# A decoder trunk on one core: the first group's products taken from x unscaled, its weights reordered, and some loads moved to ScalarE's queue

## The chip, the cores and the metric

The kernel runs on one core of a Trainium2 chip. The metric is the device time of one execution in microseconds (us). TensorE (PE) multiplies, VectorE (DVE) and ScalarE (ACT) do elementwise work, GpSimd (POOL) does a little, and SyncE (SP) issues nearly all transfers. Each engine takes its own instructions in order and waits by semaphore for what other engines and transfers give it. A transfer is issued by an engine's queue and runs on the core's 16 DMA engines.

## The reference

Two layers on x of 256 rows by 1024 columns in float32: a gated feed-forward, a mixer (pooling in the first layer, attention in the second) and a second gated feed-forward, each between two RMS norms. What is at issue here is the very first piece:

```python
def rms_norm(x, gain):
    y = x32 * lax.rsqrt(jnp.mean(x32 * x32, axis=-1, keepdims=True) + RMS_EPS) * gain
def swiglu(h, w_gate, w_up, w_down):
    return (jax.nn.silu(h @ w_gate) * (h @ w_up)) @ w_down
...
f = swiglu(rms_norm(h, g[0]), ffn_w_gate[0, 0], ffn_w_up[0, 0], ffn_w_down[0, 0])   # h = x at first
```

The norm's factor, one number for each row, can be put on the rows of x before the product or on the rows of the product after it. The gain belongs to a column of x and must be in before the product.

## The kernel before

The 256 rows are two tiles of 128 (i = 0, 1). Every float32 operand is cut into a high part (a cast to fp32r, on ScalarE) and a low part (the rest, a subtraction on VectorE); a product is three matmuls: high by high, high by low, low by high. Weights come as blocks of 1 MB, `ws[b]`, in two halves of 128x1024; a half is a "unit" and holds two K chunks of 128 rows by 512 columns. Blocks 0 and 1 are the first 512 columns of the gate's weights (units 0 to 3, for K chunks 0 to 7), blocks 2 and 3 the same columns of up's (units 4 to 7). So the first group has 2 row tiles x 8 units x 6 = 96 matmuls into four accumulators.

`opening` (L622) does this group. It puts a hand-written order on PE, DVE, ACT and SP (`manual_schedule`, L695): within an engine its instructions run as they stand in the text. Work that stands behind the block in the text is placed by the compiler's scheduler, which may slip it in between where it sees an engine idle.

- `keep_warm` (L86) issues small matmuls on zeros. WARM at L90, the four FILL at L713 to L730.
- SP's order: x tile 0, first 512 columns (L74), the first gain (L92), x tile 1, first half (L703), unit 0 in two pieces of 512 columns (L707), unit 1 (L102), the second halves of x (L710), blocks 1 and 2 (L711); block 3 when a raw buffer is free (L758). There are three raw buffers.
- For each row tile `size_x` (L634) takes the largest of 128 values of a row (L636), floors it (L639) and inverts it (L640). `rows` multiplies a half of x by that, on DVE for the first half (L645) and on ACT for the second (L647).
- `turn_gain` (L649) turns the gain into a column for each K chunk. `turn_x` (L654) transposes four K chunks of a row tile on PE, `scaled_x` (L660) multiplies them by the gain on DVE, `high_x` (L668, ACT) and `low_x` (L671, DVE) make the two parts.
- `high` (L674, ACT) and `low` (L683, DVE) make a unit's parts. Units 0 and 1 lie in the two buffers of `xyp`, the six others in the six of `hlp`.
- `products` (L687) issues the matmuls of one unit and row tile: H is high by high, X low x by high weights, W high x by low weights; each has two entries, for the unit's two K chunks.
- `rstd_of` (L198) takes the norm's factor: four squares with a sum on ACT (L193), L195 on DVE, a power on POOL. L775 multiplies it with the size again, and the gate and up read that as `q` (L304, L313).
- Behind the block come the sums for a Strassen-like scheme (L779 to L787, parts at L272 and L273), then the gate (L304) behind a table load, and then `pair` (L365): `load_form` casts its first block (`us`, L368: ACT L117, DVE L118, both 128x2048), PE multiplies it (tile g), two `xy` blocks are loaded and added (L363), and so on.

Of the kernel before, what the change touches and what calls it, by code (L numbers as in the profile page):

```python
# [19 lines left out]
P = 128  # L20
# [12 lines left out]
WARM = 26  # L33
FILL = 9, 5, 8, 4
LEAST = 1e-3
SIZE_OF = 128
# [17 lines left out]
def trunk_kernel(ctx: ExitStack, tc: tile.TileContext, x, pos, gains, pscale, ws, wq, invf, amask, pmat, icnt, out):  # L54
# [37 lines left out]
    nc.sync.dma_start(gfirst[0:KC, 0:P], gains[0].rearrange("(k p) -> k p", p=P))  # L92
# [525 lines left out]
    q0 = cp.tile([P, 2], F32, name="q_x")  # L618
# [3 lines left out]
    def opening():  # L622
# [3 lines left out]
        size = cp.tile([P, 2], F32, name="size_x")  # L626
        over = cp.tile([P, 2], F32, name="over_x")
        raws, highs, units, t, tps = [], [], [], {}, {}
        banks = [accp.tile([P, 512], F32, tag="acc", name=f"acc_b0{k}") for k in range(4)]
        gu = [banks[0::2], banks[1::2]]  # L630
        y = [sc4.tile([P, D], F32, tag="y", name=f"n_x{i}") for i in range(2)]
        H, X, W = [(0, 0, 0), (0, 1, 0)], [(1, 0, 0), (1, 1, 0)], [(0, 0, 1), (0, 1, 1)]

        def size_x(i):  # L634
            z = slice(i, i + 1)
            nc.vector.tensor_reduce(  # L636
                size[:, z], h[i][:, :SIZE_OF], axis=mybir.AxisListType.X, op=ALU.max, apply_absolute_value=True
            )
            nc.vector.tensor_scalar(size[:, z], size[:, z], LEAST, None, op0=ALU.max)  # L639
            nc.vector.reciprocal(over[:, z], size[:, z])  # L640

        def rows(i, b):
            c, z = slice(b * 512, (b + 1) * 512), slice(i, i + 1)
            if b == 0:
                nc.vector.tensor_scalar_mul(y[i][:, c], h[i][:, c], over[:, z])  # L645
            else:
                nc.scalar.mul(y[i][:, c], h[i][:, c], over[:, z])  # L647

        def turn_gain():  # L649
            tp = tpp.tile([P, 4, P], F32, tag="tp", name="tp_gain")  # L650
            nc.tensor.transpose(tp[:, 0, :KC], gfirst[:KC, :P], ident[:KC, :KC])
            nc.scalar.copy(gcol, tp[:, 0, :KC])

        def turn_x(i, b):  # L654
            tps[i, b] = tp = tpp.tile([P, 4, P], F32, tag="tp", name=f"tp_x{i}{b}")
            for c in range(4):
                k = b * 4 + c
                nc.tensor.transpose(tp[:, c], y[i][:, k * P : (k + 1) * P], ident)
# [15 lines left out]
        def high(j, k=None):  # L674

            if j == len(highs):
                pool, tag = (xyp, "xy") if j < 2 else (hlp, "hl")
                highs.append(pool.tile([P, 2, 1024], F32R, tag=tag, name="hl"))
                units.append((highs[j][:, 0], highs[j][:, 1]))
# [15 lines left out]
        with tc.manual_schedule(  # L695
# [8 lines left out]
            raw = rawp.tile([P, 2, 1024], F32, tag="raw", name="raw0")  # L704
            for k in range(2):
                c = slice(k * 512, (k + 1) * 512)
                nc.sync.dma_start(raw[:, 0, c], ws[0, :, c])  # L707
            raws.append(load_raw(raw=raw, at=1))
            for i in range(2):
                nc.sync.dma_start(h[i][:, 512:], x[i * P : (i + 1) * P, 512:])  # L710
            raws.extend(load_raw() for _ in range(2))  # L711
            turn_gain()
            keep_warm(FILL[0])  # L713
            size_x(0)
            rows(0, 0)
            turn_x(0, 0)
            size_x(1)
            rows(1, 0)
            scaled_x(0, 0)
            keep_warm(FILL[1])  # L720
            turn_x(1, 0)
            scaled_x(1, 0)
            keep_warm(FILL[2])
            high(0, 0)
            high_x(0, 0)
            high(0, 1)
            low(0, 0)
            products(0, 0, H)
            low_x(0, 0)
            keep_warm(FILL[3])  # L730
            high_x(1, 0)
            products(1, 0, H[:1])
            products(0, 0, W[:1], X)
            low(0, 1)
            products(1, 0, H[1:], W[:1])
            products(0, 0, W[1:])
            products(1, 0, W[1:])
            low_x(1, 0)
            high(1)
            rows(0, 1)  # L740
            rows(1, 1)
            low(1)
            products(1, 0, X)
            turn_x(0, 1)
            for i in range(2):
                products(i, 1, H, X)
            turn_x(1, 1)
            for i in range(2):
                products(i, 1, W)
            high(2)  # L750
            scaled_x(0, 1)
            high_x(0, 1)
# [578 lines left out]
```

## Time and profile before

| what | value |
|---|---|
| time, three runs | 946.73, 946.79, 949.97 us (median 946.79) |
| profiled execution: time, span | 947.89 us, 946.1 us |
| PE busy | 930.6 us (98%), 4513 matmuls |
| DVE busy, ACT busy, POOL busy | 744.5 us, 565.2 us, 41.3 us |
| granted TensorE clock, mean | 0.998 |

The span is what the profiler saw between the first and the last instruction; the time of the same execution is 1.8 us longer. Busy PE includes overlap of neighbouring matmuls, so idle time is better read from what an engine waits for than from the share.

### The profile page before, as it was taken

To read this page: it belongs to the slowest core of one execution; us is meant where nothing else is said; L and a number is where in the kernel's file an instruction comes from. 1 tells how busy PE (TensorE), PEld (TensorE's weight loads), DVE (VectorE), ACT (ScalarE), POOL (GpSimd) and SP (SyncE) were. 2 spreads that over 40 slices of the span, in tenths; PEclk is the share of its full clock that TensorE was granted. 3 is DMA by queue.
4 is the path that set the end of the run, shared out by engine and by line. 5 is a ranking of instruction groups with operands and counts; after the bars stand their busy time and mean duration, and the time that the engine had idled before them with its cause. 6 is when DMAs were issued, how large, how long until landed. Compare 5 with 4: busy or idle time off the path is not lost.

```text
span 946.1 us, 12009 instructions
## 1 busy us (share of the span) xinstructions
PE 930.6 (98%) x4513; PEld 767.8 (81%) x4513; DVE 744.5 (79%) x822; ACT 565.2 (60%) x692; POOL 41.3 (4%) x66
## 2 busy tenths in 40 slices
PE   8999999999999999999999999999999999999997
PEld 6878878878888888888888888888899778888885
DVE  6978897789877889878888874686187877888965
ACT  6675674656647576466657653554366766676652
POOL 1000000000100000001000000110000000000000
PEclk9999999999999999999999999999999999999999
DMA  8786976775567698675696875475333545959571
GB/s 306 255 263 199 318 260 178 266 228 201 174 197 255 217 298 267 192 250 188 167 328 156 311 248 196 147 238 171 112 103 132 191 144 167 343 134 374 152 209 44
DMA packets 56777, 202.92 MB, mean 214 GB/s; under 512 B 7496, under 2 KB 7504, under 8 KB 53904
## 3 DMA queue, kind: packets, MB, share of 16 engines
q1 hardware_dynamic: 53472, 178.83, 52.7%
q0 software_dynamic: 3248, 23.33, 12.8%
q8 instruction: 35, 0.57, 0.2%
q14 instruction: 22, 0.18, 0.0%
HBM read 178.02 MB, written 1.05 MB: 189 GB/s over the span
## 4 chain that ended last, share of the span: by engine, by line
PE 84%; DVE 7%; issue 3%; DMA 3%; ACT 2%; SPq 0%; POOL 0%; DVEq 0%; POOLq 0%; ACTq 0%
PE g L140 13%; PE st L341 12%; PE acc_d L471 12%; PE acc_b L140 7%; PE u L140 7%; PE acc_d L140 5%; PE qp L140 4%; PE kp L140 3%; PE q L341 3%; PE vp L140 3%; DMA raw<-in_ws 3%; PE acc_w L140 2%; PE acc_d L341 2%; PE acc_u L140 2%; DVE hl L111 2%
## 5 line engine op out<-in xcount | busy, mean ns | idle before, releaser
L110 ACT CAST hl<-raw 128x1024 fp32r<-128x1024 f32 x146 | 151.6, 1051 | 98.0 <-PE acc_d L140 21.9
L111 DVE TENSOR_TENSOR hl<-raw,hl 128x1024 fp32r<-128x1024 f32 x146 | 176.4, 1220 | 40.2 <-ACT hl L110 38.9
L118 DVE TENSOR_TENSOR hl_lo<-xy,hl_hi 128x2048 fp32r<-128x2048 f32 x55 | 125.9, 2290 | 63.0 <-ACT hl_hi L117 63.0
L117 ACT CAST hl_hi<-xy 128x2048 fp32r<-128x2048 f32 x55 | 105.2, 1913 | 71.0 <-PE u L140 28.2
L118 DVE TENSOR_TENSOR hl_lo<-raw,hl_hi 128x2048 fp32r<-128x2048 f32 x54 | 123.5, 2286 | 17.8 <-ACT hl_hi L117 17.6
L471 PE MATMUL acc_d<-hl,h 128*128 128x512 f32 x576 | 136.9, 392 | 0.0
L471 PEld LDWEIGHTS acc_d<-hl,h 128*128 128x128 f32 x576 | 107.2, 188 | 23.5 <-DVE acc_d L530 0.9
L117 ACT CAST hl_hi<-raw 128x2048 fp32r<-128x2048 f32 x54 | 103.3, 1913 | 26.6 <-PE st L341 9.8
L322 ACT CAST h<-htp 128x512 fp32r<-128x512 f32 (+1 forms) x48 | 26.4, 550 | 33.0 <-PE htp L320 33.0
L140 PE MATMUL acc_b<-hl,aT_m 128*128 128x512 f32 x192 | 44.8, 391 | 0.4 <-ACT aT_m L230 0.2
L140 PE MATMUL acc_d<-hl,h 128*128 128x512 f32 x192 | 44.6, 391 | 0.0
L140 PEld LDWEIGHTS acc_b<-hl,aT_m 128*128 128x128 f32 x192 | 35.7, 188 | 8.3 <-DVE aT_m L231 0.6
L341 PE MATMUL st<-hl_hi,S_m 128*128 128x512 f32 x128 | 41.9, 393 | 0.0
L140 PE MATMUL g<-hl_hi,aT_m 128*128 128x512 f32 x128 | 41.9, 393 | 0.0
L140 PE MATMUL u<-hl_hi,aT_m 128*128 128x512 f32 x128 | 41.8, 393 | 0.0
L140 PEld LDWEIGHTS acc_d<-hl,h 128*128 128x128 f32 x192 | 35.7, 188 | 7.3
L361 POOL DMA_DIRECT2D xy<-raw x22 | 19.2, 872 | 450.6 <-DVE hl_lo L118 161.2
L140 PE MATMUL qp<-hl,aT_f 128*128 128x384 f32 x192 | 37.3, 343 | 0.0
L323 DVE TENSOR_TENSOR h<-htp,h 128x512 fp32r<-128x512 f32 (+1 forms) x48 | 30.8, 641 | 4.9 <-ACT h L322 4.6
L140 PE MATMUL kp<-hl,aT_hk 128*128 128x512 f32 x144 | 34.5, 394 | 0.0
L140 PEld LDWEIGHTS qp<-hl,aT_f 128*128 128x128 f32 x192 | 32.9, 188 | 1.3 <-issue 0.9
L140 PE MATMUL vp<-hl,aT_hk 128*128 128x512 f32 x144 | 33.1, 390 | 0.0
(314 smaller groups left out, 1834.3 us busy)
## 6 DMA issues: line engine op xcount, KB each, us to landing
raw<-in_ws SPq DMA_DIRECT2D x265, 512.0 KB, 4.9
xy<-in_ws SPq DMA_DIRECT2D x44, 512.0 KB, 7.5
xy<-raw POOLq DMA_DIRECT2D x22, 1024.0 KB, 8.3
rawq<-in_wq SPq DMA_DIRECT2D x8, 768.0 KB, 4.7
gain_post<-in_gains SPq DMA_DIRECT2D x14, 256.0 KB, 7.1
gain_pre<-in_gains SPq DMA_DIRECT2D x10, 256.0 KB, 7.3
h<-in_x SPq DMA_DIRECT2D x4, 256.0 KB, 5.5
rawpm<-in_pmat SPq DMA_DIRECT2D x2, 512.0 KB, 4.6
```

The source lines that it names most:

```text
L110: nc.scalar.copy(hl[:, 0, :n], raw[:, k, :n])
L111: last["dve"] = nc.vector.tensor_sub(hl[:, 1, :n], raw[:, k, :n], hl[:, 0, :n])
L117: nc.scalar.copy(hi, raw)
L118: last["dve"] = nc.vector.tensor_sub(lo, raw, hi)
L140: last["mm"] = nc.tensor.matmul(o, l, r, start=start, stop=stop)
L322: nc.scalar.copy(d[:, 0], tp[:, :nt])
L323: nc.vector.tensor_sub(d[:, 1], tp[:, :nt], d[:, 0])
L341: nc.tensor.matmul(ps, a(z, k), u[v], start=start and k == 0 and n == 0, stop=k == 3 and n == 2, skip_group_check=not start,)
L361: nc.gpsimd.dma_start(dst, src, accum_op=ALU.add)
L471: nc.tensor.matmul(f[i][k], d[:, z], u[v][:, r], start=c == 0 and m == 0, stop=m == 2 and (own is not None or c == NF - 1), skip_group_che ...
```

## The change

The sizes and the row multiplications go, with their tiles; `turn_x` transposes x itself, and the norm's whole factor `rx` is handed to the feed-forward as `q`. The gain and the two pieces of unit 0 are issued from ScalarE's queue. Block 2 is loaded before block 1, and the order of the products is units 0, 1, 4, 5, 2, 3, 6, 7: first all that needs K chunks 0 to 3. The gain's transpose takes its PSUM buffer from another pool.

```diff
-WARM = 26
-FILL = 9, 5, 8, 4
+WARM = 22
+FILL = 7, 9, 2, 2
...
-    nc.sync.dma_start(gfirst[0:KC, 0:P], gains[0].rearrange("(k p) -> k p", p=P))
+    nc.scalar.dma_start(gfirst[0:KC, 0:P], gains[0].rearrange("(k p) -> k p", p=P))
...
-        def size_x(i):
-        def rows(i, b):
...
+        def load(b):
+            raws[b] = rawp.tile([P, 2, 1024], F32, tag="raw", name=f"raw{b}")
+            for k in range(2):
+                last["dma"] = nc.sync.dma_start(raws[b][:, k], ws[b, :, k * 1024 : (k + 1) * 1024])
...
-                nc.tensor.transpose(tp[:, c], y[i][:, k * P : (k + 1) * P], ident)
+                nc.tensor.transpose(tp[:, c], h[i][:, k * P : (k + 1) * P], ident)
...
             nc.sync.dma_start(h[1][:, :512], x[P:, :512])
+            raws[0] = rawp.tile([P, 2, 1024], F32, tag="raw", name="raw0")
+            for queue, lo, hi in ((nc.scalar, 0, 512), (nc.scalar, 512, 1024), (nc.sync, 1024, 2048)):
+                queue.dma_start(raws[0].rearrange("p k n -> p (k n)")[:, lo:hi], ws[0, :, lo:hi])
+            load(2)
             for i in range(2):
                 nc.sync.dma_start(h[i][:, 512:], x[i * P : (i + 1) * P, 512:])
+            load(1)
             turn_gain()
+            turn_x(0, 0)
             keep_warm(FILL[0])
             scaled_x(0, 0)
+            high_x(0, 0)
             turn_x(1, 0)
             scaled_x(1, 0)
+            keep_warm(FILL[1])
+            high(0, 0)
+            low_x(0, 0)
+            products(0, 0, H[:1])
             keep_warm(FILL[2])
+            high_x(1, 0)
+            low(0, 0)
+            products(1, 0, H[:1])
+            products(0, 0, X[:1])
+            keep_warm(FILL[3])
             high(0, 1)
+            low_x(1, 0)
+            products(0, 0, W[:1])
+            products(1, 0, W[:1])
             low(0, 1)
+            products(0, 0, H[1:])
+            products(1, 0, H[1:])
+            high(1)
+            products(1, 0, X)
+            products(0, 0, X[1:])
+            low(1)
             products(0, 0, W[1:])
             products(1, 0, W[1:])
             for i in range(2):
                 products(i, 1, H, X)
             for i in range(2):
                 products(i, 1, W)
+            for j in (4, 5):
                 high(j)
                 low(j)
+            load(3)
             for i in range(2):
+                products(i, 4, H, X)
+            for i in range(2):
+                products(i, 4, W)
+            for i in range(2):
+                turn_x(i, 1)
+                scaled_x(i, 1)
+                high_x(i, 1)
+                low_x(i, 1)
+            for j in (2, 3):
+                high(j)
+                low(j)
+            for i in range(2):
+                products(i, 5, H, X, W)
+            for i in range(2):
+                rstd_of(h_halves(i), f"x{i}", rx[:, i : i + 1])
+            for j in (6, 7):
+                high(j)
+                low(j)
+            for i in range(2):
+                for j in (2, 3):
                     products(i, j, H, X, W)
+            for i in range(2):
+                for j in (6, 7):
+                    products(i, j, H, X, W)
+            block_no[0] = 4
...
-    ffn(0, aT, sums, go, q=q0)
+    ffn(0, aT, sums, go, q=rx)
```

More of the change, by code (lines that the diff above doesn't have):

```diff
@@ L32 @@
 DMA_SUMS = (2, 3)
-WARM = 26
-FILL = 9, 5, 8, 4
-LEAST = 1e-3
-SIZE_OF = 128
+WARM = 22
+FILL = 7, 9, 2, 2
 EPS = 1e-6
@@ L617, in trunk_kernel @@
     rx = cp.tile([P, 2], F32, name="r_x")
-    q0 = cp.tile([P, 2], F32, name="q_x")
     aT = new_aT("x")
@@ L625, in opening @@
         gcol = cp.tile([P, KC], F32, name="gain_col")
-        size = cp.tile([P, 2], F32, name="size_x")
-        over = cp.tile([P, 2], F32, name="over_x")
-        raws, highs, units, t, tps = [], [], [], {}, {}
+        raws, highs, t, tps = {}, {}, {}, {}
         banks = [accp.tile([P, 512], F32, tag="acc", name=f"acc_b0{k}") for k in range(4)]
         gu = [banks[0::2], banks[1::2]]
-        y = [sc4.tile([P, D], F32, tag="y", name=f"n_x{i}") for i in range(2)]
         H, X, W = [(0, 0, 0), (0, 1, 0)], [(1, 0, 0), (1, 1, 0)], [(0, 0, 1), (0, 1, 1)]
-        def size_x(i):
[L635 to L640, printed above, removed]
-        def rows(i, b):
[L643 to L647, printed above, removed]
+        def load(b):
+            raws[b] = rawp.tile([P, 2, 1024], F32, tag="raw", name=f"raw{b}")
+            for k in range(2):
+                last["dma"] = nc.sync.dma_start(raws[b][:, k], ws[b, :, k * 1024 : (k + 1) * 1024])
         def turn_gain():
-            tp = tpp.tile([P, 4, P], F32, tag="tp", name="tp_gain")
+            tp = gup.tile([P, 4, P], F32, tag="gu", name="tp_gain")
             nc.tensor.transpose(tp[:, 0, :KC], gfirst[:KC, :P], ident[:KC, :KC])
@@ L674, in high @@
         def high(j, k=None):
-            if j == len(highs):
+            if j not in highs:
                 pool, tag = (xyp, "xy") if j < 2 else (hlp, "hl")
-                highs.append(pool.tile([P, 2, 1024], F32R, tag=tag, name="hl"))
-                units.append((highs[j][:, 0], highs[j][:, 1]))
+                highs[j] = pool.tile([P, 2, 1024], F32R, tag=tag, name="hl")
             c = slice(0, 1024) if k is None else slice(k * 512, (k + 1) * 512)
@@ L758, in opening @@
-            raws.append(load_raw())
-            products(1, 2, H)
-            high(3)
-            low_x(1, 1)
-            products(0, 2, W)
-            products(1, 2, W, X)
-            low(3)
-            for i in range(2):
-                products(i, 3, H, X)
-            for i in range(2):
-                products(i, 3, W)
-            for j in range(4, 8):
+            for j in (4, 5):
                 high(j)
                 low(j)
-                if j == 5:
-                    for i in range(2):
-                        rstd_of(h_halves(i), f"x{i}", rx[:, i : i + 1])
-                        nc.gpsimd.tensor_mul(q0[:, i : i + 1], rx[:, i : i + 1], size[:, i : i + 1])
+            load(3)
@@ L776, in opening @@
             for i in range(2):
-                for j in range(4, 8):
+                products(i, 4, H, X)
[13 more added lines that the diff above has]
+                rstd_of(h_halves(i), f"x{i}", rx[:, i : i + 1])
```

38 lines of the change are left out of this document (removed).

## The prediction

> **What bounds the kernel now.** I read the page first, for the size of what can be won.
>
> ```profile
> span 946.1 us, 12009 instructions
> PE 930.6 (98%) x4513; PEld 767.8 (81%) x4513; DVE 744.5 (79%) x822; ACT 565.2 (60%) x692; POOL 41.3 (4%) x66
> ```
>
> TensorE is busy nearly throughout, and the change touches only the first group. So I read the timeline from 0 to 45 us next (start, duration, engine, line, operation, then the idle time before it and what ended it). First the loads, and then each engine up to the first products:
>
> ```profile
> 0.74 1.28 ACT L652 ACT_TABLE_LOAD   x1 [0.74 <-PEq L1318]
> 0.99 2.96 PE L88 MATMUL warm<-zeros 128*128 128x128 bf16 x26 [0.99 <-DVE zeros L83]
> 1.19 0.36 SPq L92 DMA_DIRECT2D gain_first<-in_gains  x1
> 1.60 0.36 SPq L703 DMA_DIRECT2D h<-in_x  x1
> 2.00 0.90 SPq L707 DMA_DIRECT2D raw<-in_ws  x2
> 2.95 0.43 SPq L102 DMA_DIRECT2D raw<-in_ws  x1
> 3.55 0.29 DVE L636 TENSOR_REDUCE size_x<-h 128x1 f32<-128x128 f32 x1 [2.62 <-DMA h<-in_x]
> 4.08 0.69 PE L88 MATMUL warm<-zeros 128*128 128x128 bf16 x9
> 4.19 0.17 ACT L652 COPY gain_col<-tp_gain 128x8 f32<-128x8 f32 x1 [2.17 <-PE tp_gain L651]
> 4.81 0.66 PE L658 MATMUL tp_x<-ident,n_x 128*128 128x128 f32 x4
> 5.38 0.29 DVE L636 TENSOR_REDUCE size_x<-h 128x1 f32<-128x128 f32 x1 [0.64 <-DMA h<-in_x]
> 6.06 0.62 ACT L681 CAST hl<-raw 128x512 fp32r<-128x512 f32 x1 [1.71 <-DMA raw<-in_ws]
> 6.49 0.68 DVE L663 TENSOR_TENSOR sum_x<-tp_x,gain_col 128x512 f32<-128x512 f32 x1
> 6.73 0.63 PE L658 MATMUL tp_x<-ident,n_x 128*128 128x128 f32 x4 [0.98 <-ACT hl L681]
> 7.21 0.62 ACT L669 CAST aT_x<-sum_x 128x512 fp32r<-128x512 f32 x1 [0.53 <-DVE sum_x L663]
> 7.88 0.49 PE L140 MATMUL acc_b<-hl,aT_x 128*128 128x512 f32 x1
> 8.73 0.62 ACT L681 CAST hl<-raw 128x512 fp32r<-128x512 f32 x1 [0.90 <-DMA raw<-in_ws]
> 9.40 0.50 PE L140 MATMUL acc_b<-hl,aT_x 128*128 128x512 f32 x1 [1.02 <-ACT hl L681]
> 9.95 2.56 PE L140 MATMUL acc_b<-hl,aT_x 128*128 128x512 f32 x10
> ```
>
> x lands at 3.55 and 5.38 us, yet the first product runs at 7.88: the size, the row multiplication, and VectorE's order (L663 for tile 0 stands behind the row multiplication of tile 1) lie between. The second product waits for the second piece of unit 0. The chain of waits has that transfer, and the list of issues from 2.9 to 3.4 us gives unit 1's time to landing as its last number (7.0 us from 2.95, so 9.95):
>
> ```profile
> 2.47 6.23 DMA raw<-in_ws
> raw<-in_ws SPq DMA_DIRECT2D x1, 512.0 KB, 7.0
> ```
>
> Then the later part of the group, from the timeline and, in the second row, the busy times of a window (PE, PEld, DVE, ACT):
>
> ```profile
> 16.00 0.62 ACT L669 CAST aT_x<-sum_x 128x512 fp32r<-128x512 f32 x1 [1.67 <-DVE sum_x L663]
> 20.00:33.00 13.00, 13.00 (x59) 10.78 (x58) 12.55 (x17) 12.39 (x18) 1.88 (x4) 1.00 0.90 332
> 16.52 2.94 ACT L681 CAST hl<-raw 128x1024 fp32r<-128x1024 f32 x3
> 17.75 14.86 PEld L140 LDWEIGHTS acc_b<-hl,aT_x 128*128 128x128 f32 x66 [0.38 <-DVE hl L685]
> 18.22 3.49 DVE L685 TENSOR_TENSOR hl<-raw,hl 128x1024 fp32r<-128x1024 f32 x3
> 19.46 0.80 SPq L102 DMA_DIRECT2D raw<-in_ws  x2
> 27.71 1.91 ACT L117 CAST hl_hi<-raw 128x2048 fp32r<-128x2048 f32 x1
> 29.65 2.29 DVE L118 TENSOR_TENSOR hl_lo<-raw,hl_hi 128x2048 fp32r<-128x2048 f32 x1 [0.40 <-ACT hl_hi L117]
> 31.86 0.69 DVE L273 TENSOR_TENSOR S_x<-sum_x,S_x 128x512 fp32r<-128x512 f32 x1
> 32.65 0.19 PEld L140 LDWEIGHTS g<-hl_hi,aT_x 128*128 128x128 f32 x1
> 33.10 0.39 PE L140 MATMUL g<-hl_lo,aT_x 128*128 128x512 f32 x1
> 50.83 0.19 PEld L341 LDWEIGHTS st<-hl_hi,S_x 128*128 128x128 f32 x1 [0.71 <-ACT hl_hi L117]
> ```
>
> From 17.75 TensorE is dense at 14.86/66 = 0.225 us a product and reaches the next group (tile g) at 32.65. But DVE and ACT are nearly full beside it: the low part that g's second product reads is done at 29.65 + 2.29 = 31.94, only 1.2 us ahead of its use at 33.10, and at 50.83 TensorE does wait for ACT. So **two chains run side by side**: TensorE's, and the casts and subtractions. The change must win on both.
>
> **The change part by part.** All times are on the clock of the profiled execution.
>
> *Issues.* Three leave SP and go to ACT. ACT's issue is in no row; SP's lasts 0.36 to 0.45 us. Three such, 1.1 to 1.35, with the table load's 1.28 end by 0.74 + 2.6 = 3.4, inside the 2.17 us that ACT waits now ahead of its copy at 4.19. So they cost nothing while that wait covers them; if the table load came first, the pieces would leave at 2.02 and on, no earlier than now. On SP everything behind moves up by 0.4 (x tile 1) to 1.3 us (unit 1). All these bytes still share the engines, so I give only part: first piece at 5.7 (now 6.06; ends 5.2 and 6.06), second at 8.2 (now 8.70; ends 7.8, by its 0.9 earlier issue, and 8.70), unit 1 at 9.6 (now 9.95; ends 8.65 and 9.95), x tile 1 at 5.4 (ends 4.97 and 6.06, the latter if it takes turns with the first piece).
>
> [...]
>
> *Front.* Warm-up: 22 x 2.96/26 = 2.50 us, to 3.5. The gain's transpose and copy, then x tile 0 transposed 3.8 to 4.45 (0.66), L663 to 5.2, L669 to 5.85, unit 0's first cast to 6.5. **First product at 6.5**, not 7.88. Tile 1: transposed to 6.05, DVE to 6.8, ACT 6.85 to 7.45. Fillers (0.69/9 = 0.077 us each, 26 before, 20 after) lie in these waits. Five of unit 0's products come before the second piece (8.2, cast to 8.85), seven after: 8.85 + 7 x 0.225 = 10.45. Before, the twelve end at 9.95 + 10 x 0.225 = 12.2. So 1.75 us are won here.
>
> *Units 1 and 4.* Unit 1's cast ends at 9.6 + 1.05 = 10.65 (1.05 from casts of its size, 2.94/3 back to back); 24 products to 16.05. Casts and subtractions of units 4 and 5 (0.98 and 1.16 each) run ahead of it.
>
> *The second half of x.* Here is the new order's weak point. Its eight transposes come only now, 16.05 to 17.25, and in ACT's and DVE's order units 2 and 3 stand behind them: L663 16.7 to 17.4, L669 to 18.05, L672 (as long as L663) to 18.75, L663 to 19.45, second L669 from 19.5. ACT has nothing from the written order between unit 5 (about 13.5) and 17.4. TensorE does unit 5 until 19.95 and then waits for unit 2's cast at 20.1 + 1.0 = 21.1: a **new wait of 1.15 us**, and 0.3 for its low part. 48 products remain: 21.1 + 0.3 + 10.8 = 32.2. TensorE alone would be 0.45 us ahead of 32.65.
>
> *ACT and DVE.* Before, from the second L669 (16.00) to the end of us's cast (29.62) ACT works 13.62 us on end, five unit casts among it. After, the same list with four: 12.64 us, from 19.5 to 32.1. The low part follows, 2.29 us, to **34.45 instead of 31.94**. The two row multiplications on ACT, the six size instructions and two multiplications on DVE and two on POOL go, but they lie ahead of 16 us, where these engines wait anyway: worth nothing beyond the front.
>
> *Sum.* g's second product moves from 33.10 to 34.5, +1.4. The chain that ends at 50.83 hangs on the low part, +2.5, less one subtraction of 0.69 that idle DVE time before can take: +1.8. I take **+1.8 us** (ends +1.4 and +2.5). The profiled execution (span 946.1, time 947.89) would be 949.7; its median companion 946.79 gives **948.6 us**. That is within 0.5%, about what a measurement of this kernel can tell from no change.
>
> **The rivals.**
>
> *B, the cast of us slips ahead (946.3).* Block 2's raw buffer comes free with unit 5, so us can be loaded near 14.6, when unit 5's subtraction is done, about 5 us ahead of the 19.46 at which its two transfers leave now, and the scheduler may put its cast into ACT's idle time before the second half of x. Then TensorE decides: -0.45 us, and no wait for us; -1.75 us if the waits for unit 2 vanished as well (945.0). For it: two buffers of `hlp` are free then. Against: before, ACT waits 1.67 us ahead of 16.00 and took nothing from behind the block.
>
> [...]
>
> *D, the change doesn't do what it says (949.0).* The pieces of unit 0 land when they do now. Then the second cast ends at 9.35, unit 0 at 10.95, unit 1's cast at 11.0, and all behind is 0.4 us later: +2.2. [...]
>
> **How the numbers follow.** Forecast 0.52, B 0.28, D 0.12, C 0.08. The range, 945.5 to 950.5, takes in B with most of its further gain, D, the forecast's own ends (948.2 to 949.3) and C; outside lie the rest of B's gain and a second slow stretch. More than 0.5% faster (under 942.1) would need more than all idle of the group: 0.01. More than 0.5% slower (over 951.5) is C twice: 0.04. The rest, 0.95, is no change. The likeliest sign is slightly slower.
>
> **What would show it.** Right: a first product near 6.5, x's second transposes near 16, TensorE waiting about 1 us for unit 2's cast (L681) near 20, and waiting for L118 ahead of g until about 34.5, with ACT's table load and gate between the block's last cast and us. B: us's cast ahead of units 6 and 7. [...] D: the wait for the second piece of unit 0 still ending at 8.7. Wrong: g starting before 32.6 with no wait, or the wait at 50.83 not moved by what g moved.

## The result and the profile after

The changed kernel is **slower** by 0.6%, clear of the noise: 953.51 us (median of 6 runs, 951.62 to 955.37) against 947.96 us (6 runs, 946.73 to 949.97), a ratio of 1.0059 [1.0047, 1.0071]. A second measurement on another chip gave 954.18 us, 1.006 [1.0038, 1.0081]. The forecast was 948.6 us with a range up to 950.5, and it put 0.95 on no change within 0.5%. The likeliest sign that it named and the place were right, the size was not: +5.6 us in place of +1.8.

The page of the changed kernel, its span and the busy row of TensorE:

```profile
span 950.5 us, 11976 instructions
...
PE 932.9 (98%) x4503; PEld 768.9 (81%) x4503; DVE 742.2 (78%) x814; ACT 563.3 (59%) x690; POOL 42.0 (4%) x64
```

The profiled execution took 952.26 us, so its span is 4.4 us longer than before, while VectorE and ScalarE are busy for 2 us less than before. The time went into waits. The timeline of the changed kernel's opening (start, duration, engine, line, operation, then idle time and what ended it):

```profile
4.13 1.12 PE L642 MATMUL tp_x<-ident,h 128*128 128x128 f32 x4 [0.41 <-DMA h<-in_x]
...
5.04 0.95 PE L86 MATMUL warm<-zeros 128*128 128x128 bf16 x7
...
7.57 0.78 PE L138 MATMUL acc_b<-hl,aT_x 128*128 128x512 f32 x1
...
8.34 1.20 PE L138 MATMUL acc_b<-hl,aT_x 128*128 128x512 f32 x2
8.50 3.57 ACT L664 CAST hl<-raw 128x512 fp32r<-128x512 f32 x4 [0.27 <-DMA raw<-in_ws]
...
17.11 1.04 PE L642 MATMUL tp_x<-ident,h 128*128 128x128 f32 x8
...
18.47 0.62 ACT L653 CAST aT_x<-sum_x 128x512 fp32r<-128x512 f32 x1 [6.40 <-DVE sum_x L647]
...
20.45 0.62 ACT L653 CAST aT_x<-sum_x 128x512 fp32r<-128x512 f32 x1 [1.36 <-DVE sum_x L647]
...
22.07 1.20 PE L138 MATMUL acc_b<-hl,aT_x 128*128 128x512 f32 x4 [1.17 <-ACT hl L664]
...
25.44 2.06 POOL L199 TENSOR_TENSOR r_x<-ms_x,nhalf 128x1 f32<-128x1 f32 x1 [24.13 <-DVE ms_x L193]
...
25.88 1.28 ACT L302 ACT_TABLE_LOAD   x1
...
27.54 0.69 ACT L302 ACTIVATE s<-acc_b,r_x 128x512 f32<-128x512 f32 x1 [0.38 <-POOL r_x L199]
...
29.82 6.11 PE L138 MATMUL acc_b<-hl,aT_x 128*128 128x512 f32 x24 [1.44 <-ACT hl L664]
...
31.67 1.91 ACT L115 CAST hl_hi<-raw 128x2048 fp32r<-128x2048 f32 x1
...
33.32 0.75 DVE L310 SCALAR_TENSOR_TENSOR m<-acc_b,r_x,s 128x512 f32<-128x512 f32 x1
...
33.99 2.29 DVE L116 TENSOR_TENSOR hl_lo<-raw,hl_hi 128x2048 fp32r<-128x2048 f32 x1
...
39.17 2.29 DVE L361 TENSOR_TENSOR xy<-xy,xy 128x2048 f32<-128x2048 f32 x1
...
55.12 0.50 PE L339 MATMUL st<-hl_lo,S_x 128*128 128x512 f32 x1 [1.24 <-DVE hl_lo L116]
```

It shows the forecast's chain, each link late. ScalarE stands still for 6.40 us until x's second half is transposed (17.11); from the second L653 cast (before: 16.00, now 20.45) it works without much pause to us's cast, and us's low part ends at 33.99 + 2.29 = 36.28, against 31.94 before. TensorE has the predicted wait for unit 2 (1.17 us) and a second one that was not predicted (1.44 us at 29.82, for unit 6), and its wait behind g, at 55.12, is now for a low part (L116); before, it was for a cast (50.83).

Marks of TensorE's place serve below as a scale: transposes into the tile `htp`, which are the same work in both kernels. From the timelines, first the kernel before, then the changed one:

```profile
72.80 0.60 PE L320 MATMUL htp<-ident,m 128*128 128x128 f32 x4
...
279.81 0.60 PE L320 MATMUL htp<-ident,m 128*128 128x128 f32 x4
...
313.51 0.60 PE L320 MATMUL htp<-ident,m 128*128 128x128 f32 x4
```

```profile
76.81 0.60 PE L318 MATMUL htp<-ident,m 128*128 128x128 f32 x4
...
283.12 0.60 PE L318 MATMUL htp<-ident,m 128*128 128x128 f32 x4
...
317.66 0.60 PE L318 MATMUL htp<-ident,m 128*128 128x128 f32 x4
```

**The opening loses 4.01 us** (72.80 to 76.81). Of these, 0.70 are won back by the second mark (+3.31), and 0.84 are lost again between the second and the third (+4.15).

### The profile page after: what moved, and what is told of

The parts are those of the page before. It is cut to its first block, busy times and chain, and to the rows that moved or that the text cites. A ratio compares the mean times of both kernels' runs of the same rounds, so it can differ in the third digit from the quotient of the medians.

```text
span 950.5 us, 11976 instructions
## 1 busy us (share of the span) xinstructions
PE 932.9 (98%) x4503; PEld 768.9 (81%) x4503; DVE 742.2 (78%) x814; ACT 563.3 (59%) x690; POOL 42.0 (4%) x64
## 4 chain that ended last, share of the span: by engine, by line
PE 82%; DVE 9%; issue 4%; ACT 3%; DMA 2%; POOL 0%; DVEq 0%; SPq 0%; POOLq 0%; ACTq 0%
PE st L339 12%; PE g L138 12%; PE acc_d L469 12%; PE u L138 7%; PE acc_b L138 7%; PE acc_d L138 5%; PE qp L138 4%; PE kp L138 3%; PE vp L138 3%; PE q L339 3%; DVE hl L109 2%; PE acc_w L138 2%; PE acc_u L138 2%; DVE hl_lo L116 2%; PE acc_d L339 2%
## 5 line engine op out<-in xcount | busy, mean ns | idle before, releaser
L116 DVE TENSOR_TENSOR hl_lo<-xy,hl_hi 128x2048 fp32r<-128x2048 f32 x55 | 125.9, 2289 | 64.1 <-ACT hl_hi L115 64.1
L116 DVE TENSOR_TENSOR hl_lo<-raw,hl_hi 128x2048 fp32r<-128x2048 f32 x54 | 123.4, 2286 | 17.0 <-ACT hl_hi L115 16.8
L321 DVE TENSOR_TENSOR h<-htp,h 128x512 fp32r<-128x512 f32 (+1 forms) x48 | 30.7, 640 | 4.6 <-ACT h L320 4.1
```

What stands on the lines that cost most here:

```text
L116: last["dve"] = nc.vector.tensor_sub(lo, raw, hi)
L321: nc.vector.tensor_sub(d[:, 1], tp[:, :nt], d[:, 0])
```

## The experiments

Two readings of the opening were put to the test first. **A**: the table load and the gate, which the scheduler put ahead of the casts of units 6 and 7, decide. **B**: the chain of casts and subtractions that starts with x's second half decides, by the end of us's low part. Later a third question came up: why the medians are 1.5 to 3 us worse than the opening alone explains.

All runs in one table. "Low part" is the end of us's low part, "opening" the shift of the transposes at 72.80 us, "xy" the median time to landing, by the list of issues, of the four loads of `xy` issued near 262 us, "step" how much the shift grows between the transposes at 279.8 and those at 313.5 us. All four come from one profiled execution; times are medians (number of runs), ratios to the kernel before in the same measurement.

| kernel | time, us | ratio | low part | opening | xy | step |
|---|---|---|---|---|---|---|
| before | 947.96 (6) | | 31.94 | 0 | 4.8 | 0 |
| changed | 953.51 (6) | 1.0059 [1.0047, 1.0071] | 36.28 | +4.01 | 5.8 | +0.8 |
| changed, again (E12) | 954.18 (6) | 1.006 [1.0038, 1.0081] | 35.72 | +3.43 | 7.3 | +2.3 |
| E1 | 952.14 (5) | 1.0049 [1.0036, 1.0061] | 36.47 | +4.17 | 4.7 | 0 |
| E2 | 953.57 (5) | 1.0068 [1.0054, 1.0081] | 34.46 | +3.65 | 5.9 | +0.9 |
| E3 | 951.7 (5) | 1.0037 [1.0025, 1.005] | 33.15 | +0.86 | 7.5 | +2.5 |
| E4 | 947.07 (11) | 0.9994 [0.9985, 1.0003] | 31.46 | -0.47 | 4.9 | 0 |
| E5 | 948.88 (12) | 1.0013 [1.0002, 1.0025] | 32.85 | +0.55 | 4.8 | 0 |
| E6 | 952.77 (6) | 1.0053 [1.0038, 1.0067] | 36.79 | +4.50 | 6.4 | +1.5 |
| E7 | 949.08 (12) | 1.0009 [0.9998, 1.0021] | 31.95 | +0.01 | 4.7 | 0 |
| E8 | 950.98 (9) | 1.0028 [1.0015, 1.004] | 33.69 | +1.40 | 6.8 | +1.8 |
| E9 | 953.34 (6) | 1.0053 [1.0034, 1.0072] | 35.17 | +3.70 | 5.6 | +0.6 |
| E10 | 948.22 (12) | 1.0005 [0.9994, 1.0015] | 31.99 | +0.25 | 4.7 | 0 |
| E11 | 947.67 (12) | 0.9994 [0.9982, 1.0006] | 31.32 | -0.69 | 5.0 | 0 |
| E13 | 950.19 (11) | 1.002 [1.0011, 1.0028] | 33.13 | +1.18 | 4.8 | 0 |
| E14 | 951.18 (5) | 1.0031 [1.0019, 1.0043] | 36.08 | +4.15 | 5.1 | +0.2 |
| E15 | 950.41 (9) | 1.0032 [1.002, 1.0044] | 33.85 | +1.86 | 4.9 | 0 |
| E16 | 949.9 (12) | 1.0018 [1.0006, 1.003] | 32.36 | +0.42 | 6.8 | +2.0 |
| E17 | 952.16 (6) | 1.0041 [1.0025, 1.0057] | 35.92 | +3.67 | 4.9 | 0 |
| E18 | 949.39 (12) | 1.0013 [1.0002, 1.0024] | 33.26 | +0.96 | 4.7 | 0 |

**E1: four warm-up matmuls more.** The changed kernel with

```diff
-WARM = 22
+WARM = 26
```

> The changed kernel with 26 small matmuls at the start again in place of 22, nothing else. Theory C (slow clock in front): in the changed kernel the fillers of L86 still take 0.13 us each at 5.04 and 6.64 us and the transposes 1.06 to 1.12 us, against 0.077 and 0.66 before; with 26 they reach the next wait at 3.95 us, fillers fall to about 0.08 us, transposes to about 0.65, the first product comes some 0.7 us earlier than 7.57 and products run at 0.225 us from the first on. Time 0.8 to 1.5 us below the changed kernel's 953.5. Rival (order): the front does not matter, since ScalarE's order behind the second half of x decides; time within 0.4 us of the changed kernel's.

TensorE came to its full speed at about 5.7 us in place of 9.3 (read from durations: four transposes took 0.70 us from 5.74 us on, 1.06 from 5.79 us on in the changed kernel; two products took 1.20 us there at 8.34 and 0.71 at 9.50), and yet the twelfth product of unit 0 ended at 12.03 us against 11.83, because its second piece landed about 1 us later in this execution (its cast, which waits for it, starts at 9.47 us against 8.50). The low part and the opening did not improve. The median did, by 1.4 us, which is not clear of the noise (the intervals of the two ratios overlap). So theory C's time came out, but not by its mechanism; E16 and E17 give a likelier one.

**E2: the norm behind units 6 and 7.** The changed kernel with

```diff
-            for i in range(2):
-                rstd_of(h_halves(i), f"x{i}", rx[:, i : i + 1])
             for j in (6, 7):
                 high(j)
                 low(j)
+            for i in range(2):
+                rstd_of(h_halves(i), f"x{i}", rx[:, i : i + 1])
```

> The changed kernel with the norm's squares written behind the casts of units 6 and 7 instead of ahead of them. Theory A (what the scheduler slipped between the squares, table load and gate with its wait for POOL, delays units 6 and 7): their casts run at about 23 to 25 us instead of 28.74, TensorE's wait of 1.44 us at 29.8 goes, the group's last product ends about 1.4 us earlier; the cast of us comes no later than 31.67. Time 1.2 to 2.0 us below 953.5. Theory B (the second half of x stands too late): the waits ahead of unit 2 (1.59 us at 22.07) stay and so does ScalarE's total up to us's cast, so the low part of us still ends near 36; time within 0.6 us of 953.5.

The timeline of this run:

```profile
22.84 10.28 PE L138 MATMUL acc_b<-hl,aT_x 128*128 128x512 f32 x44 [0.25 <-DVE hl L668]
...
32.17 2.29 DVE L116 TENSOR_TENSOR hl_lo<-raw,hl_hi 128x2048 fp32r<-128x2048 f32 x1 [0.46 <-ACT hl_hi L115]
...
34.51 0.50 PE L138 MATMUL g<-hl_lo,aT_x 128*128 128x512 f32 x1 [0.94 <-DVE hl_lo L116]
```

Units 6 and 7 come in time now: TensorE runs 44 products on end and is done at 33.12 us, 2.8 us ahead of the changed kernel. It gains only 0.36 us at the opening's mark, and nothing in the time. TensorE just waits longer for the low parts, us's and then the next one, which a cast of S and two small VectorE instructions push back. A falls. But B's other half was missed too: us's low part did not stay near 36, it came 1.82 us earlier, and the opening followed by 0.36 alone. So us's low part is not the whole measure; see E9.

**E3: units 2 and 3 ahead of x's second half.** The changed kernel with

```diff
+            for j in (2, 3):
+                high(j)
+                low(j)
             for i in range(2):
                 turn_x(i, 1)
...
-            for j in (2, 3):
-                high(j)
-                low(j)
```

> The changed kernel with the casts and subtractions of units 2 and 3 written ahead of the second half of x, in ScalarE's idle 12 to 18.5 us. The order built from it also puts table load and gate behind units 6 and 7. Theory B: TensorE's waits of 1.59 and 0.70 us at 22.07 and 23.53 go, ScalarE's chain to us's cast moves up by some 2.5 to 3 us (from 31.67 to about 29), g's first product comes near 33 instead of 35.76. Time 2.5 to 4 us below 953.5, so about level with before or up to 2 us above it. Theory A alone: as much as the run with the squares last gives, 1.2 to 2.0 us.

Its timeline:

```profile
19.97 0.62 ACT L653 CAST aT_x<-sum_x 128x512 fp32r<-128x512 f32 x1 [1.36 <-DVE sum_x L647]
...
28.93 1.90 ACT L115 CAST hl_hi<-raw 128x2048 fp32r<-128x2048 f32 x1
...
30.86 2.29 DVE L116 TENSOR_TENSOR hl_lo<-raw,hl_hi 128x2048 fp32r<-128x2048 f32 x1 [0.99 <-ACT hl_hi L115]
...
33.21 0.50 PE L138 MATMUL g<-hl_lo,aT_x 128*128 128x512 f32 x1 [1.05 <-DVE hl_lo L116]
```

Two unit casts fill ScalarE's idle time, and the low part ends 3.13 us earlier than in the changed kernel (33.15 against 36.28). TensorE's place at 72.80 us moves by 3.15 (+0.86 against +4.01): one to one, as B says. TensorE's own products end at 31.71 us here, 1.3 us *earlier* than in the kernel before, and the opening is still 0.86 us slower. So **what TensorE wins in the group is worth nothing** as long as the low part comes later than 31.94. The time fell by 1.8 us only, less than expected; a later step of 2.5 us (last column; 0.8 in the changed kernel) took the rest.

**E4 and E7: the parts without the new order.** E4 is the kernel before without the sizes and row multiplications (`turn_x` reads `h`, `q=rx`); E7 is E4 with the gain and the two pieces from ScalarE's queue, by this edit:

```diff
-    nc.sync.dma_start(gfirst[0:KC, 0:P], gains[0].rearrange("(k p) -> k p", p=P))
+    nc.scalar.dma_start(gfirst[0:KC, 0:P], gains[0].rearrange("(k p) -> k p", p=P))
...
-                nc.sync.dma_start(raw[:, 0, c], ws[0, :, c])
+                nc.scalar.dma_start(raw[:, 0, c], ws[0, :, c])
```

> The kernel before with only the sizes and the row multiplications taken out (x itself is transposed, the whole factor goes to the products); loads, queues, orders and fillers as before. Forecast's front: first product 1 to 1.3 us ahead of 7.88, but the second piece of unit 0 still lands at 8.7, so 0.3 to 1 us is won, time 0.3 to 1.0 us below before. Theory that the unscaled products themselves cost (a slower path in front): 1 us or more above before.

> The kernel before without sizes and row multiplications, and with the gain and the two pieces of unit 0 issued from ScalarE's queue; orders as before. Forecast's bounds: second piece 0 to 0.9 us earlier than in the same kernel on SP's queue, time 0 to 0.9 us below that run's 947.07, so that the parts of the change without the new order win 1 to 1.8 us against before. Theory D: no gain from the queue, time within 0.5 us of 947.1, and x tile 0 or 1 later by some tenths.

The removed instructions bring the low part forward by 0.48 us and the opening by 0.47; at the end the kernel cannot be told from before. Moving the loads takes that 0.5 back in the profiled execution: the second product of unit 0 still waits for its second piece until 9.42 us (before: 9.40). E7's time, 949.08 us, lies 2 us above E4's and outside both expectations (the intervals of the two ratios overlap); the cause is open. Rival D was right about these transfers: a second issuer landed the second piece no earlier (its cast starts at 8.75 us and the product behind it at 9.42, which in E4 starts at 8.91).

**E6: the loads back on SyncE's queue in the changed kernel.**

```diff
-            for queue, lo, hi in ((nc.scalar, 0, 512), (nc.scalar, 512, 1024), (nc.sync, 1024, 2048)):
+            for queue, lo, hi in ((nc.sync, 0, 512), (nc.sync, 512, 1024), (nc.sync, 1024, 2048)):
```

(and the gain likewise.)

> The changed kernel with the gain and the two pieces of unit 0 issued from SP again, in the place that they had before. Theory D (ScalarE's queue gives nothing, and its bytes hold up x): x tile 0 lands at 3.55 us as before in place of 4.13, the first product comes at 7 to 7.6 us in place of 7.57, time within 0.6 us of 953.5. Rival (the queue is worth its issue time): the first cast of unit 0 comes 0.4 to 0.9 us later than 6.62, unit 0 ends as much later, time 0.4 to 1 us above 953.5.

Its time cannot be told from the changed kernel's. Its profiled execution shows something else: the second L653 at 19.42 us, 1 us earlier than in the changed kernel, but the low part at 36.79, later. The first has to do with unit 0's second piece, whose cast starts at 7.66 us without a wait for the load; in the changed kernel it starts at 8.50, behind such a wait. So ScalarE's queue may even have cost the new order up to 1 us in front; that rests on one execution. Why the low part is late all the same, the timeline and four windows of this run say (stretch, length, PE busy, granted clock, DMA share, GB/s):

```profile
28.79 7.68 PE L138 MATMUL acc_b<-hl,aT_x 128*128 128x512 f32 x24 [1.45 <-ACT hl L664]
```

```profile
28.00:30.00 2.00, 1.21 (x4) 1.00 0.15 61
30.00:32.00 2.00, 1.95 (x6) 0.55 0.00 0
32.00:34.00 2.00, 2.00 (x7) 0.59 0.92 317
34.00:36.00 2.00, 2.00 (x10) 1.00 0.51 207
```

The same 24 products took 6.11 us in the changed kernel. Behind a wait of 1.45 us the granted clock fell to 0.55 and 0.59 for about 4 us, and these products took 7.68 - 6.11 = 1.57 us longer. That is near the price of a slow stretch as at the start of the kernel before (an estimate: 26 warm-up matmuls in 2.96 us are 0.114 us each, 1.48 times the 0.077 of later ones, so 2.96 x 0.48 = 1.4 us). So rival C, a fall of the clock, did come here, though not in the profiled execution of the changed kernel, whose wait at the same place was 1.44 us at a clock of 1.00. In E1 that wait was 1.46 us, and the 24 products took 6.10.

**E5 and E8: two ways to shorten the chain.** E5 is E3 with WARM = 26 and the seven fillers of FILL[0] ahead of the first transpose in place of behind it; E8 is the changed kernel with x's second half ahead of unit 4's products:

```diff
+            for i in range(2):
+                turn_x(i, 1)
+                scaled_x(i, 1)
+                high_x(i, 1)
+                low_x(i, 1)
             for i in range(2):
                 products(i, 4, H, X)
             for i in range(2):
                 products(i, 4, W)
-            for i in range(2):
-                turn_x(i, 1)
-                scaled_x(i, 1)
-                high_x(i, 1)
-                low_x(i, 1)
```

> The changed kernel with units 2 and 3 cast ahead of the second half of x, 26 small matmuls at the start and the first seven fillers put ahead of the first transposes, so that TensorE works on without a gap until x is there. Theory C (slow clock in front): fillers at 0.077 us from 4.1 us on as before, transposes near 0.66, first product 6.8 or earlier; if the front adds to the chain, second half of x about 0.7 to 1 us earlier than in the run with units 2 and 3 ahead (its second cast L653 at 19.97), and time 0.5 to 1 us below that run's 951.7. Rival: the weights' landing sets the front, not the clock; L653 within 0.3 us of 19.97 and time within 0.4 us of 951.7.

> The changed kernel with the whole step for the second half of x put ahead of unit 4's products on TensorE (units 2 and 3 still behind it on ACT and DVE), so at about 14.5 us in place of 16.9. Theory B (the chain of ACT and DVE from the second half of x to the low part of us sets the time): second L653 at about 17.5 instead of 20.45, us's low part ends near 33 instead of 36.28, TensorE's wait for it near 55 moves to about 52, time 2.5 to 3.7 us below 953.5. Rival (TensorE's own waits, or transfers later on, set it): 1.2 us or less is won, what the waits of 1.59 and 0.70 us ahead of unit 2 leave.

Both move the low part (32.85 and 33.69), and the opening follows (+0.55 and +1.40). E5's expectation failed in both numbers: with TensorE at full speed from 4 us on (seven fillers took 0.56 us from 3.99 us on), its second L653 came only 0.30 us earlier than E3's (19.67), as the rival said, and its time fell by 2.8 us, mostly because E3's late step of 2.5 us is not there. E8 moves the second L653 to 18.44 us with nothing else changed in the order of casts: B again. E8's time is 1.9 us above what its opening explains, E5's 0.6 (in E5's own profiled execution, 950.99 us, the clock fell once more, to 0.72 in the window from 194 to 196 us and 0.50 from 196 to 198, behind a wait of TensorE of 1.45 us).

**E9, E10, E11: x's second half as a pair.** In the changed kernel VectorE's order alternates between the two tiles, and the second L653 waits 1.36 us for it. E9 turns and adds both tiles first; E10 is E5 with the same, E11 joins it with E8's place and E5's fillers:

```diff
             for i in range(2):
                 turn_x(i, 1)
                 scaled_x(i, 1)
+            for i in range(2):
                 high_x(i, 1)
+            for i in range(2):
                 low_x(i, 1)
```

> The changed kernel with the second half of x handled as a pair: both tiles turned and added by VectorE, then both casts by ScalarE, then both low parts, in place of tile after tile. Theory (the chain from the second half of x through ScalarE and VectorE to us's low part decides): the second cast of aT_x starts about 1.3 us earlier than 20.45 (near 19.1), us's low part ends about 1.3 us earlier than 36.28, and TensorE's wait for hl_lo follows it one to one; the time is 0.8 to 1.5 us under the changed kernel's 953.5, about 952.3. Rival (ScalarE's table load and the gate ahead of the casts of units 6 and 7 decide): the cast is earlier but us's low part stays within 0.3 us of 36.28, and the time stays at 953 to 954.

> The changed kernel with units 2 and 3 cast ahead of the second half of x, four more fillers and one more filler block ahead of x's first transpose, and the second half of x as a pair. Theory (the chain to us's low part decides): second cast of aT_x near 18.4 (19.67 without the pairing), us's low part ends near 31.6 (32.85 without it, 31.94 in the kernel before), TensorE's wait for hl_lo about 0.3 us below the kernel before, and the time level with the kernel before or up to 0.8 us below it: 947.1 to 948.0. Rival (something later than the opening takes what is won): us's low part as said, but the time stays at 948.8 or above.

> The changed kernel with the second half of x, as a pair, ahead of unit 4's products, with the added fillers, and with units 2 and 3 where the changed kernel has them. Theory (the chain to us's low part decides): second cast of aT_x at 16 to 16.5 (18.44 with the earlier place alone), us's low part ends near 31 (33.69 with the earlier place alone, 31.94 in the kernel before), and the time is 946.5 to 947.5, 0.5 to 1 us under the kernel before. Rival (below about 32 us for us's low part TensorE's own products set the end): under 0.4 us gained on the kernel before, 947.5 to 948.5.

E9's second cast came 1.0 us earlier and us's low part 1.1, but only 0.3 reached TensorE: two small VectorE instructions (L310, L321) now run ahead of the *next* low part, where the changed kernel has one, so that it ends at 38.68 us against 39.14, and of the expected 0.8 to 1.5 us of time 0.2 were won against 953.51, or 0.8 against the changed kernel in the same measurement (E12, 954.18). The chain is the sequence of big VectorE instructions, not us's low part alone. The first sum of two `xy` blocks, which stands behind the next low part, is a better measure of it (changed kernel: 39.17 + 2.29 = 41.46). In the kernel before:

```profile
35.42 2.28 DVE L363 TENSOR_TENSOR xy<-xy,xy 128x2048 f32<-128x2048 f32 x1
```

It ends 3.76 us later than there in the changed kernel, 3.36 in E2, 3.30 in E9 and 0.63 in E3, where the opening is at +4.01, +3.65, +3.70 and +0.86; us's low part is 4.34, 2.52, 3.23 and 1.21 later. E10 and E11 bring the low part to the level of before and below it. E11's timeline:

```profile
15.36 1.22 ACT L653 CAST aT_x<-sum_x 128x512 fp32r<-128x512 f32 x2 [3.00 <-DVE sum_x L647]
...
29.03 2.29 DVE L116 TENSOR_TENSOR hl_lo<-raw,hl_hi 128x2048 fp32r<-128x2048 f32 x1 [2.14 <-ACT hl_hi L115]
...
31.45 0.42 PE L138 MATMUL g<-hl_lo,aT_x 128*128 128x512 f32 x1
```

So the new order can be had without loss: E11 is 6.5 us faster than the changed kernel in the same measurement (E12) and level with the kernel before. It does not beat it, against the expectation: the 0.69 us won at 72.80 is gone by 125 us (-0.03), inside the next stages. E10, at 948.22, lies between the times that its two theories gave.

**E12: the changed kernel again.**

> The changed kernel once more, unaltered, for a value from the same chip as the three others: 952 to 955 us, 1.004 to 1.007 of the kernel before. Its opening should show the same order on ScalarE and us's low part ending within 1 us of 36.28; the distance between its two profiled executions says how much of an opening varies by itself.

Its opening is 0.6 us better than in the first profile (second L653 at 19.91 in place of 20.45) and its time 0.7 us worse. This, with E3 and E8, showed that a second cost lies beyond the opening.

**E13, E14, E15: a late opening by itself.** The kernel before with WARM = 84 and 116, and E11 with WARM = 84:

```diff
-WARM = 26
+WARM = 116
```

> The kernel before with 84 warm-up matmuls in place of 26, so that TensorE's first transposes stand about 58 x 0.077 = 4.5 us later; nothing else changes. Some of it is taken back, since the weights have landed by then: us's low part 2.5 to 4.5 us later than 31.94. Theory L (a late opening by itself costs more than its delay, by what happens at 270 to 290 us): median 1 to 2.5 us above 947.7 plus the shift read at 73 us of the span. Theory O (the surplus belongs to the changed order): median within 0.5 us of 947.7 plus that shift.

> The kernel before with 116 warm-up matmuls: first transposes about 6.9 us later, us's low part 4.5 to 7 us later than 31.94. Theory L: median 1 to 2.5 us above 947.7 plus the shift read at 73 us of the span. Theory O: within 0.5 us of 947.7 plus that shift. Either way its shift beside that of the run with 84 says what a further us of delay costs.

> The version with x's second half early and as a pair (947.67, level with the kernel before) with 84 warm-up matmuls in place of 26. us's low part 2.5 to 4.5 us later than its 31.32. Theory L: the median is 1 to 2.5 us more above 947.7 than the shift read at 73 us of the span. Theory O in the form that the changed order and a delay together bring the surplus: the same here, but not in the kernel before with the same warm-up. If neither shows a surplus, it belongs to the load order of the changed kernel at its own delay, and stays open.

E14 delays the opening as much as the change does (+4.15 against +4.01), with the low part at 36.08. It costs 951.18 - 948.26 = 2.9 us, not 5.6; 0.9 us are given back before 280 us and a step of only 0.2 follows. So L falls for a delay of the changed kernel's size: it brings no surplus. E13 and E15 cost 1.9 and 2.2 us at openings of +1.18 and +1.86, by the kernel before in the same measurement (948.26). By the 947.7 that the expectations name, E13 would be 1.3 us above its opening, within L's bounds, and E15 0.9, within neither's; so E14 decides. The surplus belongs to something in the changed kernel that E11 does not have.

**E16, E17, E18: where an instruction packet falls.** The step stands at a cast of `xy` by ScalarE that waits for its load. The DMA view of the kernel before, and of the changed kernel around the issue of that load (265.14 us; the window of the row with q8, 264.8 to 265.0 us, holds one packet alone: queue, kind, packets, MB, share), each with its cast from the timeline:

```profile
xy<-in_ws SPq DMA_DIRECT2D x4, 512.0 KB, 4.8
```

```profile
267.27 1.92 ACT L117 CAST hl_hi<-xy 128x2048 fp32r<-128x2048 f32 x1 [0.23 <-PE acc_b L140]
```

```profile
q8 instruction: 1, 0.02, 45.2%
...
xy<-in_ws SPq DMA_DIRECT2D x4, 512.0 KB, 5.8
```

```profile
271.41 1.91 ACT L115 CAST hl_hi<-xy 128x2048 fp32r<-128x2048 f32 x1 [1.05 <-DMA xy<-in_ws]
```

The packet is of 16 KB (the page of either kernel counts 35 of them, 0.57 MB) and starts 0.28 us ahead of the load's issue. Six other runs have a late xy. In E2, E3, E8 and E12 the DMA views place the packet between 0.05 and 0.55 us ahead; in E6 and E9 they show only that none starts from 0.05 us ahead of the issue to 3 us behind it. Of the other runs so far, the kernel before has it 1.56 us ahead, E1 0.5 to 0.7, E4 and E5 at least 1.1; in E7, E10, E11, E13, E14 and E15 none starts in that same stretch around the issue, and no view places it. The seven with a late xy have WARM = 22, the others 26 or more. E16 is the kernel before with 13 warm-up matmuls fewer; E17 and E18 are the changed kernel and E3 with ten small matmuls more, in a wait of TensorE:

```diff
                 for j in (6, 7):
                     products(i, j, H, X, W)
+            keep_warm(10)
             block_no[0] = 4
```

> The kernel before with 13 warm-up matmuls in place of 26: the 16 KB instruction packet that starts 1.56 us ahead of xy's issue (at 261.8 us) moves by 0.1 us for each matmul taken out, to about 0.3 us ahead. Theory F (that packet delays the load): xy lands in 5.6 to 7.5 us in place of 4.8, ScalarE waits for it, and the median is 1.5 to 2.5 us above 947.7 plus the shift read at 73 us of the span. Rival: xy lands in 4.7 to 5.1 us and the median stays within 0.7 us of that sum, wherever the packet is.

> The changed kernel with ten small matmuls on zeros as the last of TensorE's written order, in its wait ahead of g (0.8 us of matmuls in a wait of over 1 us). Shift at 73 us of the span as in the changed kernel, 3.4 to 4.1. Theory F: the packet moves from 0.2 to 0.3 us ahead of xy's issue to about 1.2, xy lands in 4.7 to 5.1 us in place of 5.8 to 7.3, and the median is 951.5 to 952.2 in place of 953.5 to 954.2. Rival: xy and the median as in the changed kernel.

> The version with units 2 and 3 ahead of x's second half (951.7, of which 0.9 us at 73 us of the span), with the same ten matmuls in the wait ahead of g. Theory F: xy lands in 4.7 to 5.1 us in place of 7.5, no step between 280 and 313 us, median 948.5 to 949.5. Rival: 951 to 952.

The DMA view and the cast in E17 (the packet's window is 263.6 to 263.9 us, the load's issue 265.07):

```profile
q8 instruction: 1, 0.02, 20.0%
...
xy<-in_ws SPq DMA_DIRECT2D x4, 512.0 KB, 4.9
```

```profile
270.51 1.92 ACT L115 CAST hl_hi<-xy 128x2048 fp32r<-128x2048 f32 x1 [0.23 <-PE acc_b L138]
```

And in E16 (packet between 262.3 and 262.5, load issued from 261.88 on):

```profile
q8 instruction: 1, 0.02, 43.4%
...
xy<-in_ws SPq DMA_DIRECT2D x4, 512.0 KB, 6.8
```

```profile
269.37 1.91 ACT L117 CAST hl_hi<-xy 128x2048 fp32r<-128x2048 f32 x1 [2.27 <-DMA xy<-in_ws]
```

In landings and times all three came out as theory F said; in E16 the packet came 0.45 us behind the load's first issue and not 0.3 us ahead of it. The kernel before with nothing but 13 small matmuls fewer gets the late load, a step of 2.0 us and 1.8 us of time at an opening of +0.42. The changed kernel with ten *more* matmuls loses the step and runs in 952.16 us (951.5 to 952.82), 1.4 to 2 us less than without them; the intervals of these ratios overlap. E3 falls from 951.7 to 949.39, and there they do not (1.0037 [1.0025, 1.005] against 1.0013 [1.0002, 1.0024]). Shown is that 13 of TensorE's matmuls fewer turned the late load on (landing in 6.8 us in place of 4.8) and ten more turned it off (4.9 in place of 5.8, and 4.7 in place of 7.5 in E18); a late opening did not bring it in E14 (+4.15 us by 90 matmuls more, landing in 5.1). That the packet itself holds the load back is not shown; only its place speaks for it. How the 0.96 to 1.45 us that one packet takes (20.0% of 16 engines in 0.3 us in E17, 45.2% in 0.2 us in the changed kernel) become a step of up to 2.5 us stays open.

The sum: the profiled execution of the changed kernel took 952.26 us, 4.37 more than that of the kernel before. These are the opening's 4.01, less 0.70 won back, 0.84 at the step and 0.22 behind it. In the second profile (E12, 953.1 us, 5.21 more) they are 3.43, less 0.59, 2.32 and 0.05. The medians are 5.6 and 6.4 us above the kernel before, so 1.2 more than each profile accounts for. The changed kernel's executions spread over 3.8 us (951.62 to 955.37), E17's, without the late load, over 1.3; that the load is later still in the slower ones would fit, but no profile shows it. E17 costs 952.16 - 948.12 = 4.0 us: about what the opening loses.

## Why the prediction was wrong

**The likeliest sign, the chain and the place were right.** The late second half of x, the wait for unit 2 (forecast 1.15 us, measured 1.17), and the low parts as what the products behind g wait for are in the profile. The two steps that failed are the size of the low part's delay and the bound of the change: the opening cost 4.0 us in place of 1.8, and a load near 265 us came late, which was no term at all. Rival B did not come (the cast of us stood behind units 6 and 7), D was right for the transfers but not for the time, and C showed up in other executions only.

**The term "us's low part at 34.45" was too small by 1.83 us** (measured 36.28). By the rows it splits in three:

- The second L669 cast, forecast at 19.5, ran at 20.45: +0.95. The forecast took TensorE's first transposes and fillers at the durations of the kernel before, 0.66 and 0.077 us each; in the changed kernel they took 1.12 us and 0.95/7 = 0.136, and TensorE was slow until about 9.3 us. x's first tile landed only for a start at 4.13 us (forecast 3.8). The first product ran at 7.57 in place of 6.5, and the twelfth ended at 11.83 in place of 10.45. (In the kernel before it ended at 12.51, not at the 12.2 of the forecast, so 0.68 us were won there in place of 1.75.) How much of the 0.95 the slow TensorE made is open: without it, E1's unit 0 ended no earlier, and E5's cast came 0.30 us earlier than E3's. The same kernel in E12 had the cast at 19.91, so more than half of the 0.95 differs between executions.
- ScalarE's stretch from there to the end of us's cast was taken as 12.64 us and lasted 33.58 - 20.45 = 13.13: +0.49. The gate waited 0.38 us for GpSimd, whose power took 2.06 us (0.86 in the kernel before).
- Between us's cast and its low part stood 0.41 us: VectorE, without a gap since 29.80, did the gate's product L310 (33.32) first.

**The credit of 0.69 us was nearly right.** The forecast's sum ended near 50.83 us. The next product there, which reads a low part, stood at

```profile
51.35 0.50 PE L341 MATMUL st<-hl_lo,S_x 128*128 128x512 f32 x1
```

and stands at 55.12 now, so 3.77 us later, 0.57 less than us's low part (4.34). With the three terms above, 1.8 + 1.85 + 0.12 = 3.77. Another 0.24 us are lost on the way to the mark at 72.80; why is open.

**TensorE's own products were forecast to end at 32.2 us and ended at 29.82 + 6.11 = 35.93**: units 2 and 3 came late, and the wait for unit 6 was not in the sum. The forecast's win of TensorE did not come in the changed kernel. It hardly counted: E2 ended these products 2.8 us earlier and won 0.36 us of the opening.

**"The change touches only the first group" failed too**, and nothing was put down for what comes later: the sum ended at 50.83 us. The change takes matmuls out of TensorE's stream (4503 against 4513), and the instruction packet near 265 us starts 0.28 us ahead of the load's issue in place of 1.56; with 13 matmuls fewer (E16) and ten more (E17) it moved as well, to 0.45 us behind and 1.35 ahead. By E17 that late load cost 1.4 to 2 us, about a quarter to a third of the loss. The opening alone already left the range (E17: 4.0 us above the kernel before, 950.8 on the forecast's base of 946.79); with it as forecast, the late load would have brought 950.0 to 950.6, the range's edge. The chance of 0.04 for more than 0.5% slower, which is what came, rested on the clock alone. How long a wait has to be for the clock to fall, no run shows, so C's chances (0.08, and 0.04 for two such stretches) were a guess: it fell behind 1.45 us in E6 and E5, the products behind 1.46 us in E1 were not slowed, and the changed kernel was at 1.00 behind 1.44.

**What the parts are worth**, by the runs: the unscaled products nothing that can be told (E4, 0.9994 [0.9985, 1.0003]), ScalarE's queue nothing that is won (E7), and the new order with its place for x's second half the opening's 4.0 us, since E11, which keeps ScalarE's queue and the order of the weights, moves that half, pairs its tiles and starts with more small matmuls, has none of it.

## What to carry to other kernels

When work is moved, follow the engine that prepares operands past the point where it idles: it lost 6.4 us ahead of x's second half, and nothing TensorE won could repay that. Ask of every reordering which big cast or subtraction ends last, not which product does. And test a small loss or gain with a few dummy matmuls more or less in a harmless wait: if the time jumps by 0.2%, as here, a loss or gain of that size need not be the idea's own.

## What the runs showed of the hardware

- A 16 KB packet of the instruction queue that started 0.05 to 0.55 us ahead of the issue of four loads of 512 KB (changed, E2, E3, E8, E12), or 0.45 us behind it (E16), went with a median landing of 5.8 to 7.5 us. In the runs without a late load (before, E1, E4, E5, E7, E10, E11, E13 to E15, E17, E18) it was 4.7 to 5.1; there no packet started from 0.05 us ahead of the issue to 3 us behind it, and in E1 one started 0.5 to 0.7 us ahead. That the packet is the cause is not shown.
- The granted clock fell to 0.55 behind a wait of TensorE of 1.45 us (E6), and stayed at 1.00 behind one of 1.44 us at the same place in the changed kernel. In E5 it fell to 0.50 behind another wait of 1.45 us. In E1 the wait at E6's place was 1.46 us, and the 24 products behind it took 6.10 us, against 7.68 in E6.
- At the start TensorE was slow while the granted clock read 1.00. In the window of the changed kernel from 4 to 6 us (length, PE busy, clock, DMA share, GB/s)

```profile
4.00:6.00 2.00, 1.86 (x12) 1.00 0.96 323
```

  seven fillers took 0.136 us each, against 0.077 for nine in the kernel before, from 4.08 us on. So in these first microseconds the durations tell TensorE's speed, and that column does not.
